# Sliding windows by DMA alone: a twelfth staged batch, and all 15-row remainders at the end on the software ring

## The chip, the cores and the metric

One core of one Trainium2 chip runs the kernel. The metric is the device time of one execution in microseconds (us), as the median of several runs. A ratio is the mean time of one kernel's fast runs over the mean of the other's fast runs of the same rounds, with a 95% interval; it is not quite the ratio of the medians quoted beside it. The calls ran on different chips: each ratio compares runs of one call, but the medians of the kernel before lie between 745.28 and 746.67 us from call to call, so whole spans of different calls can be compared only to about a microsecond.

## The reference

```
batch, length, dim = (32, 4096, 256);  window_size = 64;  stride = 32      # float32
n_windows = (length - window_size) // stride + 1                           # 127
for i in range(n_windows):
    result[:, i] = x[:, i*32 : i*32 + 64]
```

Nothing is computed. Call 32 rows of a batch a block: 32 x 256 x 4 bytes = 32 KB. A batch has 128 blocks, and window w is the blocks w and w+1, so every block but the first and the last is written twice. The input is 134 MB, the output 266 MB.

## The kernel before

There are two ways to move a batch.

- **Direct** (21 batches, on the sync engine's DMA ring): HBM to HBM, 16 windows to a transfer, seven of them, and a 15-window remainder. The DMA engines carry 8.32 MB for such a batch, and HBM reads 8.32 and writes 8.32.
- **Staged** (11 batches, on the scalar engine's ring): the batch is loaded into SBUF once (4.19 MB), then stored twice, as first halves and as second halves of windows (8.32 MB). The engines carry 12.5 MB, a half more than direct; HBM reads only 4.19 MB and writes 8.32.

So a staged batch spares HBM 4.1 MB and costs the DMA engines 4.2 MB.

```python
def windows(self, q, b, w0, n, half=None):          # direct: 64 KB per window, or one 32 KB half
    ...
    max_dma_last_dim=DIRECT)                        # pieces of 32768 bytes
def load(self, q, t, b): ...                        # 128 x 32 KB, pieces of 16384 bytes
def store(self, q, t, b, half, p0=0, n=None): ...   # n rows of 32 KB, pieces of 16384 bytes

# Staging: the last batch's store
    if g == len(self.batches) - 1:
        for half, p0, rows in ((0, 0, 112), (0, 112, 15), (1, 1, 15), (1, 16, 112)):
            self.c.count(self.c.store(q, self.tiles[i], self.batches[g], half, p0, rows))
        return
    for half in (0, 1):                             # all others: 128 rows twice
        self.c.store(q, self.tiles[i], self.batches[g], half).then_inc(self.stored[i], 16)
# Staging.run: six loads, their twelve stores, five loads, their stores
```

A 128-row store writes one half-window too many into a neighbouring batch. That neighbour's remainder must therefore wait until the store has landed, which is why it is a transfer of its own.

```python
staged = [*range(1, B - 3, 3), B - 2]
...
for i, b in enumerate(direct):
    for j in range(7):
        loading = turns < 102 or 306 <= turns < 391
        share += 5 if loading else 1
        cut = share >= 6                            # 5 of 6 halved while loading, 1 of 6 while storing
        turns += 4 if cut else 3
        if cut:
            share -= 6
            c.windows(ring_d, b, w0 + 16 * j, 16, 0)    # two transfers of 16 x 32 KB
            c.windows(ring_d, b, w0 + 16 * j, 16, 1)
        else:
            c.windows(ring_d, b, w0 + 16 * j, 16)       # one of 16 x 64 KB
    ...
    elif i >= len(free) + late:
        rest(direct[i - late])                      # remainders follow 8 batches late
for b in direct[-late:]:
    rest(b)
```

"Turns" counts packets. The Trainium skill ("DMA: Bandwidth & Descriptors", section "Queues, rings and completion order") says that each DMA engine goes round-robin over the rings that have work for it, one packet at a time. A whole transfer of 16 windows is two 32 KB packets and one 4-byte semaphore packet on each engine, 3 turns; the two halves are 4 turns for the same bytes. On most of its turns the other ring moves one 16 KB packet. Halving transfers thus shifts the mix of traffic toward the staging ring. The trace agrees: from 150 to 280 us of the span of before, the direct ring has 1517 packets (559 of them semaphores) and the staging ring 1516 (81 semaphores).

## Time and profile before

| | |
|---|---|
| time, median of the runs known before the prediction | 746.64 us (745.91 to 747.06) |
| the profiled execution | 753.78 us, span 752.0 us |
| packet bytes over the 16 engines | 313.16 MB |
| HBM read + written | 487.9 MB |

The page's span, its slices (40 equal ones; DMA in tenths of 16 engines busy, then GB/s), its packet count, its queue table (packets, MB, share of 16 engines' span) and its HBM line, for the kernel before:

```profile
span 752.0 us, 308 instructions
DMA  9999999999999999999999999999999999999997
GB/s 372 422 419 432 424 435 427 414 426 416 416 425 422 423 424 416 422 421 420 421 421 395 424 423 424 431 429 417 429 416 414 416 422 425 417 429 420 417 393 302
DMA packets 17885, 313.16 MB, mean 416 GB/s; under 512 B 4105, under 2 KB 4105, under 8 KB 4105
q1 hardware_dynamic: 8881, 174.80, 55.2%
q10 hardware_dynamic: 9002, 138.35, 44.1%
HBM read 220.92 MB, written 266.99 MB: 649 GB/s over the span
```

q1 is the direct ring, q10 the staging ring. No compute engine works; the DMA engines are 90% busy or more in 39 of the 40 slices. So time is the sum of packet times over 16 engines, plus a start and a ragged tail. The page's table of issues (number, KB each, us from issue to landing) shows the direct transfers, whole and halved, and the 21 remainders of 960 KB; below it, the sync queue's own waits show how long remainders waited for stores (us in total, times, longest):

```profile
out_dram<-in_x_dram SPq DMA_DIRECT2D x92, 1024.0 KB, 100.3
out_dram<-xb ACTq DMA_DIRECT2D x20, 4096.0 KB, 142.4
out_dram<-in_x_dram SPq DMA_DIRECT2D x110, 512.0 KB, 91.0
out_dram<-in_x_dram SPq DMA_DIRECT2D x21, 960.0 KB, 99.2
```

```profile
SPq L41 <- DMA out_dram<-xb: 63.8, 2, 41.4
```

Those waits cost nothing while 100 us of issued transfers lie ahead of the engines.

The trace also records every DMA packet (start, duration, ring, bytes). Most 32 KB direct packets take 1.213 us, most 16 KB staging packets 0.611 us, a semaphore packet 0.009 us. I call the number of packets times these durations, over 16, the **floor**, and what the recorded packets take beyond it the **excess**. In this profile the floor is 729.1 us and the excess 17.9 us.

### The profile page before, as it was taken

Reading aid. Unit: us, or ns where it says so; the run is one execution under the profiler, and the core shown is the slowest. Engines: PE = TensorE matmul, PEld = TensorE weight load, DVE = VectorE, ACT = ScalarE, POOL = GpSimd, SP = SyncE. Lnnn points to the kernel's source line nnn. Section 1 sums busy time; section 2 is a strip of 40 time slices with the busy share of each in tenths; the row PEclk is TensorE's granted clock in tenths of the full one; section 3 lists DMA queues with packets and bytes.
Section 4 is the critical chain, followed back from the end, with each engine's and each line's share of the span. In section 5 each row is a group of like instructions: output and inputs, shape, how many; then the busy total and the mean of one; then the engine's idle time right before and its main releaser. Section 6 shows DMA issues by size and latency. Waiting matters only on the chain. (4 is left out here: it accounts for less than half of the span.)

```text
span 752.0 us, 308 instructions
## 1 busy us (share of the span) xinstructions
POOL 0.2 (0%) x4
## 2 busy tenths in 40 slices
POOL 0000000000000000000000000000000000000000
DMA  9999999999999999999999999999999999999997
GB/s 372 422 419 432 424 435 427 414 426 416 416 425 422 423 424 416 422 421 420 421 421 395 424 423 424 431 429 417 429 416 414 416 422 425 417 429 420 417 393 302
DMA packets 17885, 313.16 MB, mean 416 GB/s; under 512 B 4105, under 2 KB 4105, under 8 KB 4105
## 3 DMA queue, kind: packets, MB, share of 16 engines
q1 hardware_dynamic: 8881, 174.80, 55.2%
q10 hardware_dynamic: 9002, 138.35, 44.1%
q14 instruction: 2, 0.02, 0.0%
HBM read 220.92 MB, written 266.99 MB: 649 GB/s over the span
## 5 line engine op out<-in xcount | busy, mean ns | idle before, releaser
L187 POOL MEMSET const-bfloat16-1.0<- 128x1 bf16 x1 | 0.1, 103 | 0.0
L187 POOL MEMSET const-uint8-127<- 128x1 uint8 x1 | 0.1, 102 | 0.0
L187 POOL MEMSET const-float32-0.0<- 128x1 f32 x1 | 0.1, 100 | 0.2 <-issue 0.2
L187 POOL MEMSET const-float32-1.0<- 128x1 f32 x1 | 0.1, 99 | 0.0
## 6 DMA issues: line engine op xcount, KB each, us to landing
out_dram<-in_x_dram SPq DMA_DIRECT2D x92, 1024.0 KB, 100.3
out_dram<-xb ACTq DMA_DIRECT2D x20, 4096.0 KB, 142.4
out_dram<-in_x_dram SPq DMA_DIRECT2D x110, 512.0 KB, 91.0
xb<-in_x_dram ACTq DMA_DIRECT2D x11, 4096.0 KB, 124.0
out_dram<-in_x_dram SPq DMA_DIRECT2D x21, 960.0 KB, 99.2
out_dram<-xb ACTq DMA_DIRECT2D x2, 3584.0 KB, 100.5
out_dram<-xb ACTq DMA_DIRECT2D x2, 480.0 KB, 102.1
```

Of the source, the lines that this page charges most:

```text
L187: nc = _bacc.Bacc("TRN2", target_bir_lowering=False, num_devices=1)
```

## The change

Its intent: stage one more batch, so that HBM has less to do; halve direct transfers so often that direct and staged traffic have nearly the same mix throughout; and take the remainders off the sync ring. The Trainium skill ("DMA: Bandwidth & Descriptors", section "Why a DMA increments its semaphore by 16 and not by 1") says that a 15-row transfer on a hardware ring runs on the lowest 15 engines, always the same, while the software ring starts 15 consecutive engines from a cursor that moves on. The packet records don't name the engine, but they agree: before, with all such transfers on hardware rings, has 15.1 packets in flight in place of 16.1 for some 35 us before its last 5. In the diff, cuts are marked with dots and the comments are added.

```diff
+PIECES = (32768, 16384,)
...
-    staged = [*range(1, B - 3, 3), B - 2]
+    staged = [*range(1, B - 3, 3), B - 2, 0]
...
-                loading = turns < 102 or 306 <= turns < 391
-                share += 5 if loading else 1
-                cut = share >= 6
+                at = turns % (loads + per * stores)          # 102 + 6 * 34
+                share += 12 if at < loads else 9             # of 12
...
-            if b in free:
-                rest(b)
-            elif i >= len(free) + late:
-                rest(direct[i - late])
-        for b in direct[-late:]:
-            rest(b)
+        ring_r = nc.gpsimd
+        ring_r.wait_ge(near, 16)                             # the direct ring's third last transfer has landed
+        for i, b in enumerate(sorted(rests, key=lambda b: max(waits[b], default=0))):
+            for g in waits[b]:
+                st.wait_stored(ring_r, g)
+            for w, n in rest_parts(b):                       # 15 windows, once 8 and 7
+                c.windows(ring_r, b, w, n, None, PIECES[i % 2], count_soft)
```

More of the change, by code (lines that the diff above doesn't have):

```diff
@@ L23, in __init__ @@
         self.done = tc.alloc_semaphore("done")
+        self.last = tc.alloc_semaphore("last")
+        self.last_total = 0
     def xap(self, block, dims):
@@ L33, in count, with count_last, windows @@
         self.total += 16
-    def windows(self, q, b, w0, n, half=None):
+    def count_last(self, dma):
+        dma.then_inc(self.last, 16)
+        self.last_total += 16
+    def windows(self, q, b, w0, n, half=None, piece=DIRECT, count=None):
         blk = self.blk
@@ L39, in windows @@
         off = blk if half else 0
-        self.count(
+        (count or self.count)(
             q.dma_start(
@@ L47, in windows @@
                 ),
-                max_dma_last_dim=DIRECT,
+                max_dma_last_dim=piece,
             )
@@ L92, in store @@
             for half, p0, rows in ((0, 0, 112), (0, 112, 15), (1, 1, 15), (1, 16, 112)):
-                self.c.count(self.c.store(q, self.tiles[i], self.batches[g], half, p0, rows))
+                self.c.count_last(self.c.store(q, self.tiles[i], self.batches[g], half, p0, rows))
             return
@@ L132, with first, rest_parts @@
     spilled = staged[:-1]
-    def rest(b):
-        for n in (b - 1, b + 1):
-            if n in spilled:
-                st.wait_stored(ring_d, spilled.index(n))
-        c.windows(ring_d, b, 0 if b - 1 in spilled else 112, 15)
+    waits = {b: [g for g, n in enumerate(spilled) if abs(n - b) == 1] for b in direct}
+    per, loads, stores = 6, 6 * 17, 34
+    def first(b):
+        return 0 if b - 1 not in spilled else 8 if len(waits[b]) == 2 else 15
+    def rest_parts(b):
+        if len(waits[b]) == 2:
+            return [(0, 8), (120, 7)]
+        return [(0 if b - 1 in spilled else 112, 15)]
@@ L141, with mark, count_soft @@
+    soft = tc.alloc_semaphore("soft")
+    soft_total = 0
+    near = tc.alloc_semaphore("near")
+    def mark(dma):
+        dma.then_inc(near, 16)
+    def count_soft(dma):
+        nonlocal soft_total
+        dma.then_inc(soft, 16)
+        soft_total += 16
     with tc.tile_critical():
         st.run(ring_s)
-        free = [b for b in direct if b - 1 not in spilled and b + 1 not in spilled]
-        direct = free + [b for b in direct if b not in free]
-        late = 8
-        share = turns = 0
@@ L150 @@
-        for i, b in enumerate(direct):
-            w0 = 15 if b - 1 in spilled else 0
-            for j in range(7):
-                loading = turns < 102 or 306 <= turns < 391
-                share += 5 if loading else 1
-                cut = share >= 6
-                turns += 4 if cut else 3
-                if cut:
-                    share -= 6
-                    c.windows(ring_d, b, w0 + 16 * j, 16, 0)
-                    c.windows(ring_d, b, w0 + 16 * j, 16, 1)
-                else:
-                    c.windows(ring_d, b, w0 + 16 * j, 16)
-            turns += 3 if b in free or i >= len(free) + late else 0
-            if b in free:
-                rest(b)
-            elif i >= len(free) + late:
-                rest(direct[i - late])
@@ L168 @@
-        for b in direct[-late:]:
-            rest(b)
+        turns = share = 0
+        rests = []
+        todo = 7 * len(direct)
+        for b in direct:
+            for j in range(7):
+                at = turns % (loads + per * stores)
+                share += 12 if at < loads else 9
+                if share >= 12:
+                    share -= 12
+                    turns += 4
+                    c.windows(ring_d, b, first(b) + 16 * j, 16, 0)
+                    c.windows(ring_d, b, first(b) + 16 * j, 16, 1, count=mark if todo == 3 else None)
+                else:
+                    turns += 3
+                    c.windows(ring_d, b, first(b) + 16 * j, 16, count=mark if todo == 3 else None)
+                todo -= 1
+            rests.append(b)
@@ L170 @@
+        ring_r = nc.gpsimd
[5 more added lines that the diff above has]
+                c.windows(ring_r, b, w, n, None, PIECES[i % 2], count_soft)
         ring_d.wait_ge(c.done, c.total)
+        ring_d.wait_ge(soft, soft_total)
+        ring_d.wait_ge(c.last, c.last_total)
 _INS = ['x', 'window_size', 'stride']
```

## The prediction

> **What bounds it now.** Only the 16 DMA engines work. The page's slices show DMA at 90% or more in 39 of 40; the queue table gives q1 (direct, HBM to HBM) 55.2% and q10 (staging) 44.1% of 16 engines' span. So the time is the engines' packet time plus start and tail. In the trace's packet records a 32 KB direct packet takes at least 1.213 us, a 16 KB staging packet at least 0.611, a semaphore packet 0.009. With 5334, 8444 and 4105 of them the floor is 729.1 us an engine; the recorded sum is 747.3. The excess is 8.7 us on the 32 KB packets, 9.2 on the 16 KB ones. The 32 KB excess is uneven: while the staging ring loads (35 to 135 us) those packets average 1.219 us, while it stores (150 to 400) 1.25. The stretch with few halved direct transfers asks most of HBM, so there HBM is a second, soft limit. From 722 to about 757 us only 15 packets are in flight: one engine has run dry. The 23 fifteen-row DMAs landed 15 semaphore packets each (4105 = 235x16 + 23x15); the Trainium skill ("DMA: Bandwidth & Descriptors", why a DMA increments its semaphore by 16) says a hardware-ring transfer of 15 rows uses the lowest 15 engines. That costs about 35/16 = 2 us of mean engine time, and the last 6 us are ragged.
>
> **What the change does.**
> - One more batch is staged. A direct batch passes the engines once (8.32 MB), a staged one as 4.19 MB in and 8.32 MB out. Engine bytes: 313.2 to 317.4 MB (+1.35%). HBM bytes: 487.9 to 483.8 MB (-0.85%). Packets: 4780 of 32 KB, 9812 of 16 KB (half the remainders are cut to 16 KB). Floor 739.7 us, +10.6, all on the critical path, since the engines are saturated.
> - Direct transfers are all halved in load phases and 3 of 4 in store phases (before 5 of 6 and 1 of 6). Every extra semaphore packet yields a turn to the staging ring, so store phases get nearly the load phase's mix. The 32 KB excess should fall from 8.7 to about 3 us. The 16 KB excess stays near 10.
> - The remainders go to the software ring, where by the same section the 15 engines start from a rotating cursor, so no engine runs dry early: -2 to -4 us.
> - The sync ring no longer stalls on stored batches (63.8 us in the queue's own waits); the engines were full meanwhile, so no gain.
>
> A round-robin model per engine with these packet times gives 750.9 us for before (750.2 recorded to the last packet) and 755.5 for after, +0.6%: the direct ring ends near 670 us, the software ring at 745 to 752, the staging ring last. A possibly lower excess pulls me down a little.
>
> **Predicted:** 749.5 us, range 742 to 757 (8 in 10). Faster by over 2%: 1%. Within 2%: 97%. Slower by over 2%: 2%.
>
> **What would show it.** Packet bytes near 317.4 MB, HBM 484 MB; 32 KB packets in the store phases near 1.22 us; mean rate 418 to 424 GB/s; 16 packets in flight until the last 5 to 8 us; a third queue with 19.7 MB from about 655 us.
>
> **What would make it wrong.** If the 32 KB excess comes from stores as such and not from the ratio, that gain vanishes (about 756). If software-ring packets are slower, come late, or don't rotate, the tail grows by 3 to 10 us. If the 16 KB excess falls too, it ends at about 742.

(Its times between 35 and 757 us are those of the packet records' own clock, which starts 11 us before the span.)

## The result, and the profile after

| | before | after |
|---|---|---|
| time, median | 746.5 us (745.91 to 747.06, 4 runs) | 752.6 us (752.53 to 753.82, 4 runs) |
| ratio | | 1.0086 (1.0068 to 1.0103) |
| span of the profile | 752.0 us | 750.8 us |

The range held the time, and the class (within 2%) was right. But the prediction forecast +2.9 us, and +6.1 us came. There is also a puzzle: the timed runs say 0.9% slower, and the two profiles, laid side by side, say 1.2 us faster. The same lines of the profile after, with its direct transfers and remainders from the table of issues:

```profile
span 750.8 us, 372 instructions
DMA  9999999999999999999999999999999999999995
GB/s 377 433 428 433 432 431 424 430 428 433 437 423 433 433 430 443 423 432 429 423 425 431 430 433 433 432 433 429 428 436 432 429 431 436 430 427 430 417 394 220
DMA packets 19756, 317.43 MB, mean 423 GB/s; under 512 B 5162, under 2 KB 5162, under 8 KB 5162
q10 hardware_dynamic: 9818, 150.93, 47.4%
q1 hardware_dynamic: 8608, 146.82, 45.6%
q0 software_dynamic: 1328, 19.66, 6.1%
HBM read 216.79 MB, written 267.06 MB: 644 GB/s over the span
out_dram<-in_x_dram SPq DMA_DIRECT2D x236, 512.0 KB, 87.5
out_dram<-in_x_dram SPq DMA_DIRECT2D x22, 1024.0 KB, 89.2
out_dram<-in_x_dram POOLq DMA_DIRECT2D x19, 960.0 KB, 44.3
```

The engines run faster now, about 431 GB/s on average from the second slice to the 37th against about 422, because the packets have almost no excess: 4.4 us in all. They carry 4.3 MB more (146.82 + 150.93 + 19.66 against 313.16 MB). The last slice is emptier, 220 against 302 GB/s. The timeline of GpSimd in the profile after (start, us, engine, what, number, idle before and who ended it) shows when the remainders are issued:

```profile
648.99 9.74 POOL L48 DMA_DIRECT2D out_dram<-in_x_dram  x17 [648.54 <-DMA out_dram<-in_x_dram]
663.00 0.58 POOL L48 DMA_DIRECT2D out_dram<-in_x_dram  x1 [4.27 <-DMA out_dram<-xb]
703.44 1.70 POOL L48 DMA_DIRECT2D out_dram<-in_x_dram  x3 [39.86 <-DMA out_dram<-xb]
```

The first seventeen begin 12 us before the direct ring's last packet (661 us), the last three wait 40 us for the store of batch 30. In the packet records no engine runs dry before the last 10 us of packets: the wait costs nothing there.

### The profile page after: what moved, and what is told of

Its sections match the earlier page's. It is cut to its first block, busy times and chain, and to the rows that moved or that the text cites. A ratio compares the mean times of both kernels' runs of the same rounds, so it can differ in the third digit from the quotient of the medians.

```text
span 750.8 us, 372 instructions
## 1 busy us (share of the span) xinstructions
POOL 12.2 (2%) x25
## 3 DMA queue, kind: packets, MB, share of 16 engines
q10 hardware_dynamic: 9818, 150.93, 47.4%
q1 hardware_dynamic: 8608, 146.82, 45.6%
q0 software_dynamic: 1328, 19.66, 6.1%
## 4 chain that ended last, share of the span: by engine, by line
another core or an unknown queue 92%; POOL 2%; issue 0%; POOLq 0%; SPq 0%
POOL out_dram L48 2%; POOLq L107 0%; POOLq L226 0%; SPq L165 0%
## 5 line engine op out<-in xcount | busy, mean ns | idle before, releaser
L48 POOL DMA_DIRECT2D out_dram<-in_x_dram x21 | 12.0, 577 | 692.7 <-DMA out_dram<-in_x_dram 648.5
```

The costliest lines, as they stand in the source:

```text
L48: q.dma_start(out=self.oap((b * self.nw + w0) * 2 * blk + off, [[2 * blk, n], [1, size]]), in_=bass.AP(self.x.tensor, self.x.offset + (b * ...
```

## The experiments

Theory A: two limits lie close together, the DMA engines' bytes (the floor) and HBM's traffic (taken to show as excess; what speaks for that stands under e13), and the change buys excess with floor. The rivals were that the profile misleads (B), that the software ring is what costs (C), and that the rate of halved transfers has nothing to do with the excess (D). The summary first; the columns from "floor" to "end" are from each run's profile, in us. "Idle" is unused engine time after the 600th us of the record clock, as a mean over 16 engines. "End" is from the last packet to the end of the span.

| run | median us (before beside it) | ratio (95%) | span | floor | excess: 32 KB + 16 KB | idle | end |
|---|---|---|---|---|---|---|---|
| the one profile of before | 746.5 | | 752.0 | 729.1 | 8.7 + 9.2 | 4.7 | 1.8 |
| after | 752.6 (746.5) | 1.0086 (1.0068 to 1.0103) | 750.8 | 740.0 | 0.7 + 3.7 | 5.2 | 3.3 |
| e1 before again | 745.35 (745.28) | 1.0000 (0.9988 to 1.0012) | 744.1 | 729.1 | 4.1 + 5.1 | 5.5 | 1.9 |
| e2 remainders on sync ring | 752.93 (745.28) | 1.0102 (1.0089 to 1.0115) | 751.0 | 739.9 | 0.7 + 3.2 | 7.5 | 1.8 |
| e3 old rate of halving | 760.51 (745.28) | 1.0201 (1.0180 to 1.0221) | 762.6 | 739.5 | 3.4 + 9.5 | 8.9 | 3.4 |
| e4 11 staged, rate 4/12 | 747.86 (745.28) | 1.0036 (1.0019 to 1.0052) | 745.3 | 729.3 | 2.0 + 8.1 | 3.8 | 3.8 |
| e5 11 staged, rates 12/12, 3/12 | 750.41 (745.97) | 1.0066 (1.0053 to 1.0080) | 748.6 | 729.5 | 5.7 + 7.0 | 5.0 | 3.3 |
| e6 before, one early on software ring | 745.82 (745.97) | 0.9994 (0.9980 to 1.0008) | 744.5 | 729.1 | 4.2 + 5.0 | 5.8 | 1.8 |
| e7 last store unsplit (wrong result) | 751.13 (745.97) | 1.0068 (1.0055 to 1.0081) | 749.0 | 740.1 | 1.4 + 1.5 | 4.7 | 3.4 |
| e8 before, rate 2/6 throughout | 745.52 (745.97) | 0.9991 (0.9978 to 1.0003) | 743.3 | 729.1 | 3.3 + 5.8 | 4.8 | 1.7 |
| e9 after again | 752.84 (746.67) | 1.0086 (1.0072 to 1.0101) | 751.2 | 740.0 | 0.9 + 4.0 | 5.0 | 3.4 |
| e10 11 staged, software ring early | 752.15 (746.67) | 1.0074 (1.0061 to 1.0088) | 749.7 | 729.8 | 7.1 + 6.2 | 5.1 | 3.4 |
| e11 the same, rates 10/12, 6/12 | 755.82 (746.67) | 1.0123 (1.0109 to 1.0138) | 753.9 | 729.5 | 8.8 + 10.1 | 4.0 | 3.3 |
| e12 before, one late on software ring | 747.34 (746.67) | 1.0010 (0.9993 to 1.0026) | 745.6 | 729.1 | 5.7 + 4.6 | 6.1 | 1.6 |
| e13 before, 10 staged | 749.30 (746.20) | 1.0042 (1.0029 to 1.0054) | 747.0 | 718.6 | 10.4 + 10.2 | 7.0 | 1.6 |
| e14 before, 8 late on software ring | 747.92 (746.20) | 1.0024 (1.0010 to 1.0037) | 746.6 | 729.2 | 5.7 + 5.2 | 5.7 | 2.4 |

Each span also has 2.0 us before the first packet. The records of packets overlap slightly (about 16.1 in flight where 16 engines are full), so floor, excess, idle, start and end add up to some 3 to 4 us more than the span in each row.

### e1: the kernel before, profiled again

No edit.

> The kernel before, unchanged, profiled a second time. Theory A: the one profile of before is of an execution about 7 us longer (753.8 us) than its timed runs (746.5 us), so the 18 us of packet excess read from it is too large; then the span here is 744 to 746 us and the excess over the floor of 729.1 us about 11 us, with the store phases' 32 KB packets near 1.23 us. Rival B: profiles of before always show about 752 us, because profiling slows this kernel and not the changed one; then the span is 751 to 753 us here and all runs with records are long. Times against before: ratio 1.000.

Theory A held: span 744.1 us, excess 9.3 us (lower still than the 11 expected), the 32 KB packets of the first store phase (150 to 280 us of the span) at 1.229 us where the first profile has 1.252. The slices of this second profile of before:

```profile
span 744.1 us, 308 instructions
GB/s 370 432 430 424 426 432 433 429 437 417 428 430 431 425 421 423 417 430 425 424 430 405 422 435 435 425 437 425 432 424 425 431 418 427 428 431 424 411 400 289
```

The windows view shows the difference in one stretch of a store phase, 180 to 280 us (us, POOL busy, clock, DMA share, GB/s), for the first profile of before, e1 and the change:

```profile
180.00:280.00 100.00, 0.00 (x0) 1.00 1.01 422
180.00:280.00 100.00, 0.00 (x0) 1.00 1.00 426
180.00:280.00 100.00, 0.00 (x0) 1.00 1.01 432
```

From the second slice to the 37th e1's slices average 427 GB/s where the first profile has 422. So the profile that the prediction was worked out from is of an execution 7 us longer than the ones that were timed. It is not profiling that slows this kernel: this profiled execution was a normal one, and e6, e8, e12 and e14, close relatives of before, have 9.2 to 10.9 us of excess too. Why that one execution had 17.9 stays open; e3's five runs, 757.8 to 764.4 us, show that the time of one and the same kernel can spread by 6.6 us.

The puzzle is solved with this. Against a normal execution of before the change lengthens the span by 750.8 - 744.1 = 6.7 us, close to the 6.1 of the timed runs (in e9's call, on one chip, the medians differ by 6.2). From here on, e1 is "before".

### e2: the remainders at the end of the sync ring

```diff
-        ring_r = nc.gpsimd
-        ring_r.wait_ge(near, 16)
+        ring_r = ring_d
```

> The changed kernel with the remainders at the end of the sync ring, not on the software ring. Theory A (engine time bounds, the ring matters only through the rotation): the lowest engines carry 20 shares of 64 KB where the mean is 18.75, about +3 us, and the 1.8 us GpSimd drain at the end goes, so 752 to 755 us. Rival C (the software ring is what costs the 6 us): 746 to 749 us.

752.93 us, as theory A said; rival C falls. The software ring is almost a wash here. Without it one engine is dry from 709 us of the span on (15.1 packets in flight in place of 16.1) and the idle time is 7.5 us in place of 5.2. But the end after the last packet is 1.8 us in place of 3.3. In the instruction records the difference is one line: after the last transfer the change has a GpSimd DRAIN of 1.783 us, and e2 and before have none there. (Each kernel also has a closing DRAIN of about 0.1 us a little later: 0.078 in before, 0.096 in the change.) The sync queue's waits in the change show that the kernel's end waits for it (us in total, times, longest); e2 and before have no such line:

```profile
SPq L165 <- POOLq L165: 1.6, 1, 1.6
```

So the rotation wins 2.3 us and the drain takes 1.5 of it. The ratios, 1.0102 and 1.0086, have overlapping intervals; the trace is what tells the two terms apart.

### e3: the old rate of halved transfers, still 12 staged

```diff
-                share += 12 if at < loads else 9
+                share += 10 if at < loads else 2
```

> The changed kernel with before's rate of halved transfers (5 of 6 while loading, 1 of 6 while storing), still 12 staged batches. Theory A (the excess comes from the mix of direct and staged packets, which the rate of halved transfers sets): 32 KB packets in the store phases lengthen from 1.213 to 1.23 to 1.25 us, excess grows from 4.4 to 9 to 13 us, floor unchanged at 740 us less 1 us of semaphore packets; time 754 to 760 us. Rival D (12 staged batches or the software ring took the excess away, not the rate): excess stays near 4.4 us, 751 to 753 us.

760.51 us. Rival D falls in the store phases: the 32 KB packets go from 1.213 us to 1.231 (150 to 280 us) and 1.228 (560 to 640 us) with the rate alone. But that is only 2.7 us of the sum. The larger part, which I had not expected, is in the tail. Fewer halved transfers let the direct ring finish earlier, and the staging ring is left with the last batch's stores alone. The last 508 staging packets, which are those stores, average 0.828 us in place of 0.611 and make 6.9 us of excess. In the change as it is they average 0.685 and make 2.3 us; the rest of its staging packets average 0.613. Something is wrong with the last batch's stores (see e7). This profile is of the slowest run of the kernel, so its 762.6 us are not compared with the median. Whether e3 is slower than before by more than 2% stays unclear (interval 1.0180 to 1.0221).

### e4 and e5: 11 staged batches with the rest of the change

```diff
-    staged = [*range(1, B - 3, 3), B - 2, 0]
+    staged = [*range(1, B - 3, 3), B - 2]
-                share += 12 if at < loads else 9
+                share += 4                                                       # e4
+                share += 12 if turns < 102 or 306 <= turns < 391 else 3          # e5
```

> The changed kernel with 11 staged batches as before, 4 of 12 transfers halved throughout (so that the direct ring ends early enough for the remainders), remainders on the software ring. Theory A: the floor falls by 10.4 us to about 729.6 us, the excess rises to 8 to 14 us as the mix asks more of HBM; time 742 to 748 us. Rival C (software ring costs 6 us over before): 752 us or more.

> As e4 (11 staged batches, remainders on the software ring), but all transfers halved while the staging ring loads and 3 of 12 while it stores. A candidate. Theory A: the floor stays at 729.4 us, the excess of the load phases (e4: about 4.8 us of its 10.3) falls to about 2, the store phases stay below 1.5, the last batch's stores keep 2 to 3: sum 735 to 737 us, time 743 to 746 us. Rival C (software ring and its tail eat whatever the mix gives): 747 us or more, as e4.

e4 took 747.86 us: 5 us better than the change, and still no better than before. The floor fell to 729.3 us as expected and the excess rose to 10.1. In the store phases the packets are at their best (1.214 and 0.611 us from 150 to 280 us), in the load phase they are not (16 KB at 0.636 us from 20 to 90 us, where before has 0.620).

e5 missed its range (743 to 746) at 750.41. It fell where rival C had put it (747 us or more). The load phases came out as planned: 0.77 us of 16 KB excess in the first 100 us in place of e4's 2.37. What went wrong is the end. The direct ring held out to 666 us of the span, the remainders came only then, the staging ring was done at 719 us, and the last remainders ran alone to 745. Direct traffic alone asks the most of HBM per byte that an engine carries (each byte is read and written there), and there the packets are far from their floor: 1.50 us for 32 KB and 0.76 for 16 KB on average from 719 to 729 us of the span, with all 16 engines busy. The windows view of that stretch (us, POOL busy, clock, DMA share, GB/s):

```profile
716.00:730.00 14.00, 0.00 (x0) 1.00 1.01 351
```

The engines are full and move 351 GB/s instead of 430. From 719 to 729 us the records hold nothing but direct packets, and these read and wrote 695 GB/s of HBM. A limit other than the engines holds here; that it is HBM's bandwidth is inferred, for the profile has no counter of HBM's waits. The Trainium skill ("HBM Reference", specifications) gives about 716 GB/s for the memory that two cores share, and says a core alone is bounded at about 425 GB/s by its 16 DMA engines. The first fits these 695 GB/s. The second is a little low: these runs show 430 to 435 GB/s where only the engines limit.

### e6, e12 and e14: what the software ring costs at the end

e6 sends one remainder, of the last batch, to the software ring early; e12 the last of all, late; e14 the eight late ones, gated as in the change. All are before otherwise. The edit of e14, cut (the semaphores and the line that marks the third last direct transfer are left out):

```diff
-        for b in direct[-late:]:
-            rest(b)
+        nc.gpsimd.wait_ge(near, 16)
+        for b in direct[-late:]:
+            for n in (b - 1, b + 1):
+                if n in spilled:
+                    st.wait_stored(nc.gpsimd, spilled.index(n))
+            c.windows(nc.gpsimd, b, 0 if b - 1 in spilled else 112, 15)    # counted on a semaphore of its own
```

> Before with one of its 21 remainders (the last batch's, not waiting for any store) on the software ring. The disputed cost by itself: a GpSimd drain at the end, 1.8 us in the changed kernel's trace and absent in before. Theory A: it is a fixed cost of using the software ring once: the drain shows 1.7 to 1.9 us, time +1.5 to +2.2 us against before. Rival: the drain cleans up after 21 transfers and is shorter for one: below 0.5 us, time +0 to +0.5 us.

> Before with one remainder on the software ring, issued when the last but one remainder has landed, so it is among the last transfers of all. After e6, which showed no drain for an early transfer: theory G, the 1.78 us GpSimd drain stands at the end when a software-ring transfer landed shortly before the end, even for one. Expected: the drain shows again, 1.7 to 1.9 us. Rival H, the drain grows with the number of software-ring transfers: below 0.5 us. The time itself also has this transfer's own latency at the end, 748 to 755 us.

> Before with its 8 late remainders on the software ring, gated to the end of the direct ring; 13 stay where they were. Theory A: engine 15 goes dry later (7 of its 22 missing shares come back, 17 us of one engine, 1 us of the mean); if the drain grows with the number of transfers it is below 1 us here. Time 744.5 to 746.5 us against 745.3 to 746.7. Rival: the drain is 1.78 us from a few transfers on and the tail gets ragged: 747 us or more.

My theory (a fixed cost of using the ring at all) fell with e6, and the next one (only late transfers leave a drain) fell with e12. The drain after the last transfer grows with the number of transfers:

```
GpSimd DRAIN after the last transfer, from the instruction records
before, e2        0 software-ring transfers   no such DRAIN
e6  (early)       1                           0.137 us
e12 (late)        1                           0.142 us
e14               8                           0.722 us
after, e10       21                           1.78 us
```

That is about 0.08 us for each transfer ((1.783 - 0.137) / 20). With e10, whose transfers are spread over the whole run, the drain is the same 1.78 us, so in these runs neither the time nor the size of the packets mattered (e10's are all of 32 KB, half of the change's remainders are cut to 16 KB).

e6 and e12 leave the time where it was (0.9994 and 1.0010, both intervals contain 1); e12's 747.34 us is a little below my range.

e14 was to show whether the rotation pays without the drain. It took 747.92 us, outside my range and on its rival's side in time: the drain is smaller than the rival said, but the idle time at the end did not fall (5.7 us against 5.5). One engine is dry for a shorter time, but the engines now stop at different times in the last 12 us (5.1 us of idle there, against 3.5 in e1), and while both direct-type rings run at once, from 704 to 716 us of the span, their packets lengthen (averages over 2 us lie between 1.23 and 1.36 us).

### e7: the last batch's stores not split

```diff
-            for half, p0, rows in ((0, 0, 112), (0, 112, 15), (1, 1, 15), (1, 16, 112)):
-                self.c.count_last(self.c.store(q, self.tiles[i], self.batches[g], half, p0, rows))
+            for half in (0, 1):      # 128 rows; second halves one window late (new parameter): wrong on purpose
+                self.c.count_last(self.c.store(q, self.tiles[i], self.batches[g], half, shift=half))
```

> The changed kernel, wrong on purpose: the last staged batch is stored in two DMAs of 128 rows (second halves one window late) in place of 112, 15, 15 and 112 rows. In the changed kernel the last 508 staging packets average 0.685 us, the others 0.613. Theory E (the row split makes them slow): they fall to 0.611 to 0.62 us, 2 us of excess goes and the time falls to 750 to 751.5 us. Rival F (being last, or the place they are written to, makes them slow): they stay near 0.68 us and the time at 752.6 us.

Theory E held for the packets. The last 508 staging packets fell from 0.685 to 0.614 us and their excess from 2.3 to 0.1 us. It is the row split (112, 15, 15, 112) that makes those packets slow here, not their being last. The split alone is not enough, though: e1 has it too, and its last 508 packets average 0.621 us beside that kernel's traffic. Part of the gain was lost elsewhere: the 32 KB excess went from 0.7 to 1.4 us, so the whole excess fell by 1.5. The time, 751.13 us at ratio 1.0068, agrees in direction, but its interval overlaps that of the change. How the split does it was not tried. A possible reason: the Trainium skill ("SBUF — State Buffer", section "Door 1: The DMA port swizzle") says that DMA bandwidth depends on how many of the 16 SBUF ports the partitions reach, and four neighbouring partitions share a port; "DMA: Bandwidth & Descriptors" (section "The descriptor swizzle") gives each engine a port of its own in a transfer into 128 partitions. With 112 or 15 rows engines may meet on a port. No run here shows the ports.

### e8: before with an even rate

```diff
-                share += 5 if loading else 1
+                share += 2
```

> Before with 2 of 6 transfers halved throughout (5 of 6 while loading and 1 of 6 while storing before), nothing else. Theory A (the rate alone sets the excess): the store phases' 32 KB packets fall from 1.22 to 1.24 to below 1.22 us as in e4 (3 us less), the load phases' 16 KB packets lengthen (2 us more); floor unchanged at 729 us; time 742 to 746 us. Rival D (the rate hardly matters, 12 staged batches and the order of batches took the excess away in the changed kernel): store phases stay at 1.22 to 1.24 us.

745.52 us, ratio 0.9991 with 1 inside the interval. As expected the store phases got better (32 KB at 1.218 us from 150 to 280 us, against 1.229) and the load phase worse (16 KB at 0.636 from 20 to 90 us, against 0.620), and the excess is 9.2 us as in e1, only elsewhere. With 11 staged batches the rate moves the excess between phases; it does not take it away.

### e9: the change again

No edit.

> The changed kernel, unchanged, beside the others of this call. Packet excess 4 to 5 us again, last 508 staging packets near 0.685 us, GpSimd drain 1.78 us, ratio 1.007 to 1.010 against before.

All as expected: ratio 1.0086 again, excess 4.9 us, drain 1.78 us, last packets 0.681 us.

### e10 and e11: candidates with the software ring early

11 staged batches; the line with the wait on `near` taken out, so that each remainder goes as soon as its neighbours have landed; all pieces of 32 KB; rates 12/12 and 9/12 (e10) or 10/12 and 6/12 (e11).

> A candidate to beat both: 11 staged batches; the remainders on the software ring as soon as their neighbours' stores have landed, not gated to the end, all in 32 KB packets; all transfers halved in load phases, 9 of 12 in store phases, so that the direct ring lasts as long as the staging ring. Theory A: floor 729 us and excess about 9 us as in before, no engine dry from 710 us on (2 us won through the rotation), no drain at the end (last remainder lands some 30 us before it): time 742.5 to 744.5 us, ratio 0.996 to 0.998. Rival C (the software ring costs something wherever it is used much): 745 us or more.

> As e10 with fewer halved transfers (10 of 12 in load phases, 6 of 12 in store phases): the direct ring ends some 20 us before the staging ring. Theory A: the mix asks more of HBM for longer and less in the tail: excess 9 to 12 us, last batch's stores slower, 744 to 747 us.

Both missed, 752.15 and 755.82 us, on rival C's side of the line. Each landing store releases two remainders at once, and while they run two rings carry direct traffic beside one that carries staged traffic. In e10's burst from 652 to 667 us of the span, the 32 KB packets average 1.30 us on the software ring and 1.27 on the sync ring and the 16 KB ones 0.643, then fall back to 1.22 and 0.61 until the next pair. The average mix was that of before; the mix of the moment was not, and excess came to 13.3 us. Ten such bursts fill 156 us and hold 9.7 us of it. My "no drain" was wrong as well, as told above. The slices of e10 show the dips:

```profile
GB/s 378 434 434 434 423 423 440 421 433 395 424 424 418 439 405 432 424 418 438 406 429 417 406 428 433 432 430 430 429 428 421 431 407 435 425 418 430 408 409 224
```

The Trainium skill ("DMA: Bandwidth & Descriptors", section "Issuing engines are not separate DMA queues") says that issuing from several engines only saves the time to issue, since all run on the same 16 DMA engines. e2 agrees (the change with two rings or three takes the same time within 1.2 us). e10 adds a warning: another ring is another seat in the round-robin, and so changes the mix (from 654 to 665 us, 78 packets on the software ring, 92 on the sync ring and 87 on the staging ring).

### e13: the other direction, 10 staged batches

```diff
-    staged = [*range(1, B - 3, 3), B - 2]
+    staged = [*range(1, B - 6, 3), B - 2]
-                share += 5 if loading else 1
+                share += 0
```

> Before with 10 staged batches (batch 28 direct) and no halved transfers; nothing else. The floor falls to about 718.7 us. Theory A (two nearly equal limits: engine bytes and HBM traffic; 492 MB at the 672 GB/s seen in the densest stretches is 732 us): the 10 us of floor come back as excess, 20 us or more, 32 KB packets near 1.26 us or longer through all store phases; time 744 to 752 us. Rival I (only engine bytes count): excess stays near 10 us, time 735 to 738 us, a version that beats both.

749.30 us. The floor fell by 10.5 us, and all of it and more came back as excess (9.3 to 20.7, +11.4), with 32 KB packets at 1.239 us through both store phases. Its idle time is longer as well, 7.0 us, as the direct ring finishes alone. Rival I falls. This run completes the table that the whole argument rests on:

| staged batches | floor | excess | sum of packet times |
|---|---|---|---|
| 10 (e13) | 718.6 | 20.7 | 739.3 |
| 11 (e1) | 729.1 | 9.3 | 738.4 |
| 12 (after) | 740.0 | 4.4 | 744.4 |

From 10 to 11 the excess pays for the floor. From 11 to 12 there are only 9.3 us of excess left to win, and the floor costs 10.9. The rows differ in rates and rings too. The floor does not depend on those by more than 0.7 us. The excess does: with 12 staged it is 12.9 us at the old rate (e3), with 11 it lies between 9.2 (e8) and 18.9 (e11), and 10 was tried at one rate only. So the excess column shows the best rate tried for 12, close to the best for 11, and the only one for 10.

Is the excess HBM's doing? The packet records of the first store phase (150 to 280 us of the span) speak for it. HBM traffic is here the bytes of the packets, counted twice for HBM to HBM:

| kernel | 32 KB packets, us | engines, GB/s | HBM traffic, GB/s |
|---|---|---|---|
| after | 1.213 | 432 | 660 |
| e4 | 1.214 | 431 | 673 |
| e8 | 1.218 | 431 | 672 |
| e5 | 1.228 | 428 | 672 |
| e1 | 1.229 | 427 | 671 |
| e3 | 1.231 | 427 | 672 |
| e13 | 1.239 | 423 | 671 |

The engines' rate falls as direct traffic gains in share, but HBM traffic stays at 671 to 673 GB/s: it looks like a ceiling, and the change lies below it. Still, this is no proof, and it is not the whole excess. Direct traffic alone reached 695 GB/s (e5), and some stretches have excess at less traffic: e1 from 396 to 414 us moves 399 GB/s with 627 GB/s of HBM traffic, and the change from 708 to 726 us, in the last batch's split stores (see e7), moves 388 with 596. There something else must add to it; for the stretch in e1 no run isolates it.

## Why the prediction was right or wrong

It was wrong in size: +2.9 us forecast, +6.1 measured. Two steps failed. Idle engine time was to fall by 2 to 4 us, as the rotation keeps every engine fed, and fell by 0.3; and the end after the last packet, which it did not count, grew by 1.4 us through the GpSimd drain. Together that is about 4 us, the whole gap between its sum and the measured one. Its terms against those of e1 and after:

| term | predicted | measured |
|---|---|---|
| floor | +10.6 | +10.9 (729.1 to 740.0) |
| excess | -5.7 on 32 KB packets, about +1 on 16 KB ones | -3.4 and -1.4 (9.3 to 4.4 in all) |
| idle engines at the end | -2 to -4 | -0.3 (5.5 to 5.2) |
| from the last packet to the end | 0, not mentioned | +1.4 (1.9 to 3.3) |
| sum | about +3 | +7.1 by the terms, +6.7 in the span |

- **What bounds the kernel, and that the added bytes lie on the critical path**: right. The floor rose as computed, packet bytes came to 317.4 MB and HBM traffic to 483.9 MB, and the time followed the floor. The sync ring's waits for stores are gone, and nothing was won by that, as the prediction said.
- **"The 32 KB excess should fall from 8.7 to about 3 us. The 16 KB excess stays near 10"**: the direction was right, and e3 and e8 show that the rate of halved transfers moves the 32 KB excess. The sizes are right only in sum, by luck. After the change both nearly vanish (0.7 and 3.7). And before, a normal execution has 4.1 and 5.1 (e1), not 8.7 and 9.2. Had I foreseen the real packets of after, I would have forecast from that one profile -13.5 us of excess, and a faster kernel. The check that would have caught it was at hand: the profiled execution took 753.78 us and the timed runs 746.6.
- **"so no engine runs dry early: -2 to -4 us"**: this is one step that failed. No engine runs dry early now, and inside the changed kernel the rotation is worth 2.3 us (e2 against after). But before, with its engine dry for some 40 us, stops more evenly otherwise (3.5 us of its 5.5 us idle are in the last 12 us), while the change ends ragged: all of its 5.2 us are in the last 12. The dry engine was exchanged for a loose end. Why the engines of the change stop so unevenly was not tried. The model had the staging ring finish last; in the trace the software ring did, 2.7 us later.
- **The missing term**: the GpSimd drain of 1.783 us, which before does not have, of which +1.4 shows in the end term. The prediction doesn't mention it. It grows with the number of software-ring transfers (e6, e14, after).
- **"A possibly lower excess pulls me down a little"**: the model's own +0.6% (751.1 us on the timed runs of before) was nearer than the 749.5 I wrote. The excess was lower than assumed, but so was that of before.
- **The last batch's split stores**, 2.3 us of the change's remaining 4.4 us of excess (e7), were in neither list. Before they cost 0.3 us (e1): beside its traffic they mattered little.

What would have to be true for the change to win is now plain: before would need more than 11 us of excess to give up. It has 9.3.

None of the tried versions beats before. e8 and e6 are level with it (0.9991 and 0.9994, both intervals contain 1).

Open: why one execution of before had twice the excess; how the split rows slow the last stores; what the excess is outside the store phases; and whether a paced software ring (one remainder at a time, early) would avoid the bursts of e10.

## What to carry to other kernels

When two limits lie close together (here the bytes that the DMA engines carry and, as far as the traces tell, the traffic that HBM takes), write the time as a floor of undisturbed packet times plus an excess. A change that trades one for the other can win at most the excess there is, so measure that in more than one profile, and first compare the profiled execution's time with the timed runs. When several rings share engines round-robin, look at the mix of the moment (e10), and count what a further ring costs at the end: here about 0.08 us for each transfer on the software ring.

## What the Trainium skill lacked or had wrong

- No page that I read has the cost of the software ring at the end of a kernel: after the last transfer GpSimd had a drain of 0.14 us with one transfer on that ring, 0.72 with eight and 1.78 with twenty-one, early or late, and none without that ring. It belongs in "DMA: Bandwidth & Descriptors".
- "DMA: Bandwidth & Descriptors" ("Issuing engines are not separate DMA queues") says that issuing from several engines only saves issue time. The page tells of the round-robin elsewhere, but this section doesn't say that a further ring changes its shares: in e10 bursts on a third ring lengthened 32 KB packets from 1.22 to about 1.30 us and hold 9.7 of the kernel's 13.3 us of excess.
- "DMA: Bandwidth & Descriptors" has no packet time for HBM-to-HBM copies, nor how they fare beside other traffic. Here 32 KB packets of that kind take 1.213 us when mixed with enough staged traffic (430 to 435 GB/s over 16 engines) and about 1.5 us alone (about 350 GB/s, 695 GB/s of HBM read and written).
- "SBUF — State Buffer" and "DMA: Bandwidth & Descriptors" don't give the cost of stores of 112 or 15 partitions: their 16 KB packets took 0.621 us on average beside e1's direct traffic, 0.685 at the end of the change and 0.828 in e3, where the sync ring had run dry 90 us before the first of them, against 0.614 with 128 partitions (e7).
